# Output projection to first MLP product: four chunks ahead of the last weight tile, scale on VectorE, earlier transposes, squares put off

## The chip, the cores and the metric

The kernel runs on one core of a Trainium2 chip. The metric is the time of one execution on the device in microseconds (us), median of three runs; lower is better. The core has five engines, each with an in-order queue of its own: TensorE (PE; its weight loads are listed as PEld), VectorE (DVE), ScalarE (ACT), GpSimd (POOL) and SyncE (SP). The last three also issue DMA transfers.

## The reference, cut to what matters

One decoder layer over 1024 tokens of width 1024, float32, without batch. Three token mixers come first and are merged; the change touches only what follows them: the output projection with its residual, the norm, and the first of two MLP products.

```python
h = h + einsum('bsd,de->bse', merged, w_out)          # 1024 x 1024
hn = rms_norm(h, norm_mlp_g)                           # h * rsqrt(mean(h*h) + eps) * g
up = relu(einsum('bsd,df->bsf', hn, w_mlp_up))         # 1024 x 4096
h = h + einsum('bsf,fd->bsd', up * up, w_mlp_down)     # 4096 x 1024
return rms_norm(h, final_norm_g)
```

## The kernel before, in words

**Precision.** Every float32 product is made of three products of rounded parts: a tile is split into a high part (ScalarE, line 132) and the rest (VectorE, line 133: source minus high part), and TensorE runs high x high, high x low and low x high. So a "split" of a 128 x 1024 tile is one ScalarE and one VectorE instruction. The products are 128 x 512 matmuls into one PSUM bank.

**Order.** Inside `with tc.manual_schedule():` the program order is the order of every engine's queue. What an engine does next is therefore fixed by where the line stands in the program, whether its input is there or not. Waits between engines, and for buffers, are put in by the framework. A tile of a pool can be written once the last reader of the tile that had the buffer before is done. The pools that matter: `act2` (27 buffers of 128 x 1024, `act()`), `act3` (16), `w` (6), `raw` (2, for weights as they are loaded), `aux` and `aux2` (4 PSUM banks each).

**Output projection** (`out_products`, line 1387). The tokens are 8 chunks of 128, the output has two halves `nb` of 512 columns. A chunk and a half take 8 steps k of 3 matmuls, 24 in all. The weights of a half are four tiles `wo_make(nb, k2)` of two k each; a tile is loaded by SP into a raw buffer, and each `wo_make` also starts the load of the tile two further on. The first three tiles of half 0 are split while the merge before still runs; `wo_make(0, 3)` comes after the merge's own last work on ScalarE and VectorE. The first half goes by pairs of chunks: for the first pair k = 0..5 of both chunks, then the fourth tile is split, then k = 6, 7 of both; the three other pairs follow whole, and behind each pair one tile of half 1 is split (`wo_make(1, cp)`) and the products are added to the residual `H[c]` (line 1408). `residual(c)` loads a chunk of x; its DMA is issued on ScalarE's queue, two chunks at the start and two with each later pair.

**Second half, norm and transposes** (lines 1645 to 1667). For each chunk c: half of its matmuls; the transpose of chunk c - 2 (`transpose_plain`: eight 128 x 128 transposes on TensorE into two PSUM banks, line 1431, and eight ScalarE copies out of them with the norm's gain, line 1436); the other matmuls; for c = 5 and 6 the forms B11 and B21; the sum into `H[c]` (line 1656); `norm_scale`; the store of `H[c]` to `h_d` by POOL. `norm_scale` squares and sums the row on ScalarE (line 1414), takes the inverse root in nine tiny VectorE instructions (lines 107 to 112) and scales the row on ScalarE (line 1422). A "form" is a pair of 128 x 1024 tiles that hold a quarter of the transposed normed tokens, or a sum of quarters, and their split (`form`).

**First MLP product.** The hidden width is 16 blocks s of 2 x 128 columns. A block is a 2 x 2 product over halves of the tokens and of the inner width, done with seven products instead of eight: `p1 p2 p5 p6 p3 p7 p4`, each 12 matmuls (`seventh`, line 487). The left factors come from `Weights` (`cast1`: A11, A12; `cast12`: S1, S2; `cast34`: S3, S4; `cast22`: A22; `sums1`, `sums2` form S on VectorE, lines 511 to 516), the right ones are the forms B11, B21, B22, T1, T2, T3, T4. The products depend on one another through PSUM: p6 adds to the bank of p1, which ScalarE must have copied out before (line 1475); p3 adds to that of p5 (copy on line 1494), p7 to that of p6 (line 1498), and p4 to that of p7, whose sum VectorE must have taken (line 1509). The results lie in `o0` and `o1`, are passed through relu and a square on ScalarE (`square_relu`, lines 1452 and 1453) and stored by POOL to `u_d` together with sums of them (`sums` and `last_sum` on VectorE, lines 1515 to 1527); `last_sum` of block s comes behind p4, at the start of block s + 1.

Block 0 is done without the seven products: `plain` (line 1639) runs 24 matmuls four times (two columns, two halves of the tokens). The first token half needs B11 and B21, the second B12 and B22. Its work, and block 1, are woven by hand into the stretch in which the other forms are made:

1. plain (column 0, half 0), S sums of block 1, transpose of chunk 6
2. plain (1, 0), `cast12`, squares and store of block 0's first half, transpose of chunk 7
3. block 1's p1, forms B12 and B22, T1 difference, p2, form T1, T2 difference
4. plain (0, 1), form T2, squares of block 1's first quarter, `cast34`, T3 difference
5. plain (1, 1), form T3, T4 difference, p5, form T4, p6, first casts of block 2, squares of block 0's second half
6. p3, S sums of block 2, p7, `cast12` of block 2, block 0's sums and their stores, block 1's sums

Then the loop over s = 2..15 runs block s with p4 of block s - 1 behind its p1, and the next block's casts between its products. The second MLP product reads `u_d` back from s = 15 on.

Of the kernel before, what the change touches and what calls it, by code (L numbers as in the profile page):

```python
# [19 lines left out]
KD = D // P  # L20
# [16 lines left out]
def trunk_kernel(ctx: ExitStack, tc: tile.TileContext, x, norm_mix_g, w_in, b_gate, gmlp_ln_g, gmlp_ln_b,  # L37
# [1350 lines left out]

    with tc.manual_schedule():
        for cp in range(NCH // 2):  # L1390
            pss = [aux(), aux()]
            if cp:
                for i in range(2):
                    residual(2 * cp + i)
            if cp == 0:
                for i in range(2):
                    out_products(pss[i], 0, i, range(6))
                wo_make(0, 3)
                for i in range(2):
                    out_products(pss[i], 0, i, (6, 7))  # L1400
                wo_make(1, 0)
            else:
                for i in range(2):
                    out_products(pss[i], 0, 2 * cp + i, range(KD))
                wo_make(1, cp)
            for i in range(2):
                h = H[2 * cp + i]
                tt(out=h[:, hsl(0)], in0=pss[i], in1=h[:, hsl(0)], op=ALU.add)
# [10 lines left out]
    def norm_scale(row):  # L1419
        xn = act()  # L1420
        rs = row_rms(row, xn)
        actv(xn, row, AF.Identity, scale=rs)
        return xn
# [31 lines left out]
    class Super:  # L1455
# [33 lines left out]

        def p5(self):  # L1490
            self.b2 = aux()
            self.mul(self.b2, "S1", "T1", True)
            self.o1 = act()
            actv(self.o1[:, hsl(1)], self.b2, AF.Copy)  # L1494
# [5 lines left out]
        def p3(self):  # L1500
# [3 lines left out]
            square_relu(c)  # L1504

        def p7(self):
# [3 lines left out]
            square_relu(c)  # L1510
# [134 lines left out]
    with tc.manual_schedule():  # L1645

        xns, weights = [], {}
        for c in range(NCH):
# [4 lines left out]
            out_products(ps, 1, c, range(4, KD))  # L1653
            if c in (5, 6):
                form(("B11", "B21")[c - 5], quad(0, c - 5), act3)
            tt(out=H[c][:, hsl(1)], in0=ps, in1=H[c][:, hsl(1)], op=ALU.add)
            xns.append(norm_scale(H[c]))
            nc.gpsimd.dma_start(out=h_d[c], in_=H[c])
# [7 lines left out]
            elif c == 7:  # L1666
                weights[1].cast1()
        z0, z1 = Super(0, None), Super(1, weights[1])
# [4 lines left out]
        transpose_plain(xns[6], 6)  # L1673
        plain(z0, 1, 0, w0[1])
        weights[1].cast12()
        for o in (z0.o0, z0.o1):
            actv(o[:, hsl(0)], o[:, hsl(0)], AF.Square)
        z0.store(("A11",), z0.o0[:, hsl(0)])
        transpose_plain(xns[7], 7)
        z1.p1()  # L1680
        n11, n12, n21, n22 = quad(0, 0), quad(1, 0), quad(0, 1), quad(1, 1)
# [4 lines left out]
        for j in range(2):  # L1686
            tt(out=T1[j], in0=n12[j], in1=n11[j], op=sub)
        z1.p2(False)
        form("T1", T1, act3)
        for j in range(2):  # L1690
            tt(out=T2[j], in0=n22[j], in1=T1[j], op=sub)
        plain(z0, 0, 1, w0[0])
        form("T2", T2, act3)
        z1.square_first()
        weights[1].cast34()
        for j in range(2):
            tt(out=n12[j], in0=n22[j], in1=n12[j], op=sub)
        plain(z0, 1, 1, w0[1])
        form("T3", n12, act)
        for j in range(2):  # L1700
            tt(out=n21[j], in0=n21[j], in1=T2[j], op=sub)
        weights[2] = Weights(w_up, 4 * P, w4)
# [5 lines left out]
        for o in (z0.o0, z0.o1):  # L1708
            actv(o[:, hsl(1)], o[:, hsl(1)], AF.Square)
        z1.p3()  # L1710
        weights[2].sums1()
        weights[2].sums2()
        z1.p7()
        weights[2].cast12()
        z0.sums()
        z0.last_sum()
        z1.sums()
        weights[3] = Weights(w_up, 6 * P, w4)
        prev = z1
        dn = dn_steps()  # L1720
        for s in range(2, NS):
# [11 lines left out]
            prev.last_sum()  # L1733
# [23 lines left out]
            if last:  # L1757
                advance(dn)
            z.p7()
            if last:  # L1760
                advance(dn)
            z.sums()
            if s + 2 < NS:
# [101 lines left out]
```

## Time and profile before

| | |
|---|---|
| runs | 1957.18, 1958.79, 1960.37 us; median 1958.79 |
| profiled execution, first to last instruction | 1959.5 us, 0.7 over the median of the runs |
| mean granted TensorE clock in it | 0.991 |
| TensorE busy in it | 1905.2 us (97%) |
| VectorE, ScalarE, POOL busy | 1410.2, 1014.1, 259.3 us |

| stretch, us from the span's start | what runs | TensorE idle |
|---|---|---|
| 0 to 1212 | input projection, mixers, merge | 22.0 |
| 1212 to 1261 | output projection, first half | 2.8 |
| 1261 to 1315 | second half, norm, transposes 0 to 5 | 2.8 |
| 1315 to 1388 | plain products, blocks 1 and 2, forms | 8.3 |
| 1388 to 1927 | rest of the first MLP product, second one | 1.8 |
| 1927 to 1959.5 | last products, final norm, output | 16.6 |

The profiled execution's own time is its span; the runs' times are taken apart from it. In the rows, a line of the timeline gives the start, the length, the engine, the program line, the operation, what it writes and reads, the count, and in brackets the idle time before it with what ended it. Tiles are named by their pool: `a` is `act2`, `b` is `act3`, `wt` and `wb` are `w`, `rt` is `raw`. A matmul of 512 columns is listed with about 389 ns, but a new one starts every 227 ns at the full clock; a listed busy stretch of TensorE ends some 0.16 us after the next instruction could have started.

### The profile page before, as it was taken

The page shows a single profiled execution, that of the slowest core. Times are in us where ns is not written, and L with a number is a line of the kernel's source. Part 1 is how long each engine was busy: PE and PEld are TensorE (multiplying, and loading weights), DVE is VectorE, ACT ScalarE, POOL GpSimd, SP SyncE. Part 2 cuts the span into 40 slices and gives each one's busy share as a digit, 9 for nine tenths or more (in the row PEclk, how much of TensorE's full clock was granted, in tenths as well). Part 3 has the DMA queues.
Part 4 walks back from the last instruction along what each step waited for, and adds up shares of the span by engine and source line. Part 5 has one row for each costly group of instructions (what it writes and reads, how often), then busy time and mean ns, then how long its engine had stood idle before and what let it go on. Part 6 is the DMA issues. An engine that isn't in the chain of part 4 may idle for free.

```text
span 1959.5 us, 23757 instructions
## 1 busy us (share of the span) xinstructions
PE 1905.2 (97%) x8928; PEld 1587.5 (81%) x8928; DVE 1410.2 (72%) x2039; ACT 1014.1 (52%) x1471; POOL 259.3 (13%) x355
## 2 busy tenths in 40 slices
PE   8999999999999999999999999998999999999996
PEld 7998878888887787878778887877788887888885
DVE  6585869788758767677777888248655567688787
ACT  6435959676534545454554544167555556243253
POOL 3112112122342010100010110000211110000000
PEclk9999999999999999999999999999999999999998
DMA  4346475576754343434497986331544448453532
GB/s 162 75 137 145 110 153 122 121 164 138 169 142 136 107 151 108 151 108 129 149 287 256 279 220 194 107 108 54 199 139 167 154 172 294 164 172 118 183 119 86
DMA packets 211015, 301.25 MB, mean 154 GB/s; under 512 B 13028, under 2 KB 125876, under 8 KB 210900
## 3 DMA queue, kind: packets, MB, share of 16 engines
q1 hardware_dynamic: 167348, 158.54, 26.4%
q0 software_dynamic: 34544, 119.69, 22.8%
q10 hardware_dynamic: 9008, 21.51, 3.1%
q8 instruction: 70, 1.15, 0.3%
q14 instruction: 45, 0.37, 0.1%
HBM read 195.75 MB, written 74.58 MB: 138 GB/s over the span
## 4 chain that ended last, share of the span: by engine, by line
PE 74%; DVE 9%; issue 6%; ACT 5%; DMA 5%; POOL 1%; ACTq 0%; POOLq 0%; DVEq 0%; SPq 0%
PE aux L487 39%; PE ps L564 14%; PE gps L487 10%; PE aux L257 4%; PE aux L1387 2%; PE aux L800 1%; DMA a<-acs_d 1%; DMA c<-yc_d 1%; ACT a L1436 1%; DMA raw<-in_w_in_dram 1%; PE aux L736 1%; PE aux L732 1%; DVE a L133 1%; DVE rsq_q L111 1%; ACT a L132 1%
## 5 line engine op out<-in xcount | busy, mean ns | idle before, releaser
L564 PE MATMUL ps<-xn,wh 128*128 128x512 f32 x1088 | 295.0, 392 | 0.0
L487 PE MATMUL aux<-b,b 128*128 128x512 f32 x1152 | 264.4, 389 | 1.0 <-DVE b L133 0.9
L487 PEld LDWEIGHTS aux<-b,b 128*128 128x128 f32 x1152 | 216.0, 188 | 47.0 <-DVE b L133 1.8
L564 PEld LDWEIGHTS ps<-xn,wh 128*128 128x128 f32 x1088 | 202.9, 188 | 42.2 <-issue 0.9
L487 PE MATMUL aux<-a,b 128*128 128x512 f32 x960 | 219.4, 389 | 0.0
L487 PEld LDWEIGHTS aux<-a,b 128*128 128x128 f32 x960 | 180.2, 188 | 37.4
L564 PE MATMUL ps<-xn,wl 128*128 128x512 f32 x544 | 168.2, 389 | 0.0
L487 PE MATMUL gps<-xn,wt 128*128 128x512 f32 x684 | 160.2, 392 | 2.1 <-DVE a L238 2.1
L487 PE MATMUL aux<-b,wt 128*128 128x512 f32 x672 | 156.9, 389 | 0.0
L487 PEld LDWEIGHTS gps<-xn,wt 128*128 128x128 f32 x684 | 129.4, 189 | 29.5 <-issue 2.5
L487 PEld LDWEIGHTS aux<-b,wt 128*128 128x128 f32 x672 | 126.1, 188 | 26.2
L132 ACT ACTIVATE b<-wt 128x1024 fp32r<-128x1024 f32 x88 | 90.8, 1052 | 86.4 <-DMA wt<-u_d 51.9
L133 DVE TENSOR_TENSOR wt<-a,wt 128x1024 fp32r<-128x1024 f32 x66 | 80.8, 1225 | 66.9 <-ACT wt L132 66.9
L564 PEld LDWEIGHTS ps<-xn,wl 128*128 128x128 f32 x544 | 102.1, 188 | 21.4
L133 DVE TENSOR_TENSOR b<-wt,b 128x1024 fp32r<-128x1024 f32 x88 | 107.1, 1218 | 15.8 <-ACT b L132 15.8
L1617 DVE TENSOR_TENSOR a<-aux,a 128x512 f32<-128x512 f32 x112 | 76.9, 687 | 50.2 <-PE aux L487 50.2
L133 DVE TENSOR_TENSOR a<-a,a 128x1024 fp32r<-128x1024 f32 (+1 forms) x68 | 66.6, 985 | 41.5 <-ACT a L132 41.5
L133 DVE TENSOR_TENSOR wt<-rt,wt 128x1024 fp32r<-128x1024 f32 x35 | 42.8, 1224 | 57.2 <-ACT wt L132 57.0
L132 ACT ACTIVATE a<-a 128x1024 fp32r<-128x1024 f32 (+1 forms) x68 | 55.9, 837 | 54.1 <-DVE a L1569 45.9
L487 PE MATMUL aux<-a,wt 128*128 128x512 f32 x336 | 78.7, 390 | 3.3 <-ACT a L1494 3.3
L487 PEld LDWEIGHTS aux<-a,wt 128*128 128x128 f32 x336 | 62.9, 188 | 17.2 <-ACT a L1494 4.2
L132 ACT ACTIVATE wt<-a 128x1024 fp32r<-128x1024 f32 x66 | 69.6, 1055 | 8.7 <-DVE a L515 8.3
(349 smaller groups left out, 3521.2 us busy)
## 6 DMA issues: line engine op xcount, KB each, us to landing
wt<-u_d SPq DMA_DIRECT2D x54, 512.0 KB
u_d<-a POOLq DMA_DIRECT2D x48, 512.0 KB, 5.3
raw<-in_w_in_dram SPq DMA_DIRECT2D x34, 512.0 KB
wl<-raw POOLq DMA_DIRECT2D x34, 512.0 KB, 5.1
g_d<-a POOLq DMA_DIRECT2D x24, 512.0 KB, 3.3
a<-g_d ACTq DMA_DIRECT2D x24, 512.0 KB
rt<-in_w_in_dram SPq DMA_DIRECT2D x19, 512.0 KB
a<-in_w_in_dram SPq DMA_DIRECT2D x19, 512.0 KB
```

Of the source, the lines that this page charges most:

```text
L111: stt(out=q, in0=r, scalar=nh, in1=r, op0=ALU.mult, op1=ALU.mult)
L132: actv(dst_hi, src, AF.Copy)
L133: (eng or nc.vector).tensor_tensor(out=dst_lo, in0=src, in1=dst_hi.bitcast(F32), op=ALU.subtract)
L257: mm(ps[:, :nt], X.tok(a, k, c), wk[k][w], start=(k == 0 and i == 0), stop=(k == KD - 1 and i == 2))
L487: mm(ps, lhs[l][kk], rhs[r][kk], start=(new and n == 0), stop=(n == 11), skip_group_check=not new)
L564: mm(ps[:, hsl(h)], w[wi][:, k, :], a.rhs(ai, k, h), start=(n == 0), stop=(n == 3 * KD - 1))
L732: mm(yo[:, tok(i)], pv[c // 2][:, c % 2, j * P:(j + 1) * P], Cf[:, tok(c)], start=True, stop=True)
L736: mm(yi[64 * h:64 * h + 64, tok(i)], xdt[c // 2][:, c % 2, 2 * j + h, :], E[c // 2][:, c % 2, 2 * j + h, :], start=True, stop=True)
L800: mm(ps, w[wi][:, q * P:(q + 1) * P], S["xs"][half][ai], start=(n == 0), stop=(n == 2))
L1387: mm(ps, M.tok(a, k, c), wo[nb][k][w], start=(k == 0 and a + w == 0), stop=(k == KD - 1 and a == 1))
L1436: actv(Nf[th, k // 2][:, k % 2, (c % 4) * P:(c % 4 + 1) * P], ps[:, i * P:(i + 1) * P], AF.Identity, scale=g2c[:, KD + k:KD + k + 1])
L1617: tt(out=h, in0=ps, in1=h, op=ALU.add)
```

## The change

- First half of the projection: residual chunks 2 and 3 are loaded at once. k = 0..5 runs for four chunks, then `wo_make(0, 3)`, then k = 6, 7 of each of the four with its sum and the load of residual c + 4; then `wo_make(1, 0)`; chunks 4 to 7 follow singly, with `wo_make(1, 1..3)` ahead of the sums of chunks 4 to 6.
- `norm_scale`: the scaling by the inverse root is a VectorE `tensor_scalar` instead of a ScalarE activation.
- Second half: sum, norm and store stand ahead of the forms B11 and B21. Transpose 6 moves ahead of the first plain product, transpose 7 ahead of the second.
- Block 1: the forms B12 and B22 and the T1 difference come ahead of p1; T1, T2 and `cast34` ahead of plain (0, 1); T3 and the T4 difference ahead of plain (1, 1).
- The squares of blocks 0 and 1, the store of A11 of both, and both blocks' `sums` and `last_sum` leave the stretch. A generator `catch_up` gives them out in six parts, two in each of the blocks s = 2, 3 and 4: one ahead of p7, one behind `sums`. Only p4's own relu and square of block 1 stay where they were.

```diff
@@ -1386,26 +1386,28 @@
             for a, w in ((0, 0), (0, 1), (1, 0)):
                 mm(ps, M.tok(a, k, c), wo[nb][k][w], start=(k == 0 and a + w == 0), stop=(k == KD - 1 and a == 1))
 
+    def add_half(c, nb, ps):
+        tt(out=H[c][:, hsl(nb)], in0=ps, in1=H[c][:, hsl(nb)], op=ALU.add)
+
     with tc.manual_schedule():
-        for cp in range(NCH // 2):
-            pss = [aux(), aux()]
-            if cp:
-                for i in range(2):
-                    residual(2 * cp + i)
-            if cp == 0:
-                for i in range(2):
-                    out_products(pss[i], 0, i, range(6))
-                wo_make(0, 3)
-                for i in range(2):
-                    out_products(pss[i], 0, i, (6, 7))
-                wo_make(1, 0)
-            else:
-                for i in range(2):
-                    out_products(pss[i], 0, 2 * cp + i, range(KD))
-                wo_make(1, cp)
-            for i in range(2):
-                h = H[2 * cp + i]
-                tt(out=h[:, hsl(0)], in0=pss[i], in1=h[:, hsl(0)], op=ALU.add)
+        for c in (2, 3):
+            residual(c)
+        pss = [aux() for _ in range(4)]
+        for c in range(4):
+            out_products(pss[c], 0, c, range(6))
+        wo_make(0, 3)
+        for c in range(4):
+            out_products(pss[c], 0, c, (6, 7))
+            add_half(c, 0, pss[c])
+            residual(c + 4)
+        wo_make(1, 0)
+        for c in range(4, NCH):
+            ps = aux()
+            out_products(ps, 0, c, range(KD))
+            if c < 7:
+                wo_make(1, c - 3)
+            add_half(c, 0, ps)
+    del pss, ps
 
     Nf = {}
 
@@ -1419,7 +1421,7 @@
     def norm_scale(row):
         xn = act()
         rs = row_rms(row, xn)
-        actv(xn, row, AF.Identity, scale=rs)
+        ts(out=xn, in0=row, scalar1=rs, scalar2=None, op0=ALU.mult)
         return xn
 
     def transpose_plain(xn, c):
@@ -1487,6 +1489,10 @@
             square_relu(c)
             self.store(("A11",), c)
 
+        def square_rest(self):
+            square_relu(self.o0[:, hsl(1)])
+            square_relu(self.o1[:, hsl(1)])
+
         def p5(self):
             self.b2 = aux()
             self.mul(self.b2, "S1", "T1", True)
@@ -1497,17 +1503,19 @@
             self.mul(self.b1, "S2", "T2", False)
             actv(self.o0[:, hsl(1)], self.b1, AF.Copy)
 
-        def p3(self):
+        def p3(self, square=True):
             self.mul(self.b2, "S4", "B22", False)
             c = self.o0[:, hsl(1)]
             tt(out=c, in0=self.b2, in1=c, op=ALU.add)
-            square_relu(c)
-
-        def p7(self):
+            if square:
+                square_relu(c)
+
+        def p7(self, square=True):
             self.mul(self.b1, "S3", "T3", False)
             c = self.o1[:, hsl(1)]
             tt(out=c, in0=self.b1, in1=c, op=ALU.add)
-            square_relu(c)
+            if square:
+                square_relu(c)
 
         def sums(self):
             self.s12, self.s34 = act(), act()
@@ -1651,11 +1659,11 @@
             if c >= 2:
                 transpose_plain(xns[c - 2], c - 2)
             out_products(ps, 1, c, range(4, KD))
+            add_half(c, 1, ps)
+            xns.append(norm_scale(H[c]))
+            nc.gpsimd.dma_start(out=h_d[c], in_=H[c])
             if c in (5, 6):
                 form(("B11", "B21")[c - 5], quad(0, c - 5), act3)
-            tt(out=H[c][:, hsl(1)], in0=ps, in1=H[c][:, hsl(1)], op=ALU.add)
-            xns.append(norm_scale(H[c]))
-            nc.gpsimd.dma_start(out=h_d[c], in_=H[c])
             if c == 0:
                 w0 = plain_weights()
             elif c in (1, 2):
@@ -1665,59 +1673,69 @@
                 weights[1] = Weights(w_up, 2 * P, act)
             elif c == 7:
                 weights[1].cast1()
+        transpose_plain(xns[6], 6)
         z0, z1 = Super(0, None), Super(1, weights[1])
         z0.o0, z0.o1 = act(), act()
         plain(z0, 0, 0, w0[0])
         weights[1].sums1()
         weights[1].sums2()
-        transpose_plain(xns[6], 6)
+        transpose_plain(xns[7], 7)
         plain(z0, 1, 0, w0[1])
+        n11, n12, n21, n22 = quad(0, 0), quad(1, 0), quad(0, 1), quad(1, 1)
         weights[1].cast12()
-        for o in (z0.o0, z0.o1):
-            actv(o[:, hsl(0)], o[:, hsl(0)], AF.Square)
-        z0.store(("A11",), z0.o0[:, hsl(0)])
-        transpose_plain(xns[7], 7)
-        z1.p1()
-        n11, n12, n21, n22 = quad(0, 0), quad(1, 0), quad(0, 1), quad(1, 1)
         form("B12", n12, act)
         form("B22", n22, act)
         T1 = [act((P, 2, HF)) for _ in range(2)]
         T2 = [act((P, 2, HF)) for _ in range(2)]
         for j in range(2):
             tt(out=T1[j], in0=n12[j], in1=n11[j], op=sub)
+        z1.p1()
+        form("T1", T1, act3)
         z1.p2(False)
-        form("T1", T1, act3)
         for j in range(2):
             tt(out=T2[j], in0=n22[j], in1=T1[j], op=sub)
+        form("T2", T2, act3)
+        weights[1].cast34()
         plain(z0, 0, 1, w0[0])
-        form("T2", T2, act3)
-        z1.square_first()
-        weights[1].cast34()
         for j in range(2):
             tt(out=n12[j], in0=n22[j], in1=n12[j], op=sub)
-        plain(z0, 1, 1, w0[1])
         form("T3", n12, act)
         for j in range(2):
             tt(out=n21[j], in0=n21[j], in1=T2[j], op=sub)
+        plain(z0, 1, 1, w0[1])
         weights[2] = Weights(w_up, 4 * P, w4)
         z1.p5()
         form("T4", n21, act)
         z1.p6()
         weights[2].cast1()
         weights[1].cast22()
-        for o in (z0.o0, z0.o1):
-            actv(o[:, hsl(1)], o[:, hsl(1)], AF.Square)
-        z1.p3()
+        z1.p3(False)
         weights[2].sums1()
         weights[2].sums2()
-        z1.p7()
+        z1.p7(False)
         weights[2].cast12()
-        z0.sums()
-        z0.last_sum()
-        z1.sums()
         weights[3] = Weights(w_up, 6 * P, w4)
+
+        def catch_up():
+            z1.square_first()
+            z1.square_rest()
+            yield
+            z1.sums()
+            z1.last_sum()
+            yield
+            for o in (z0.o0, z0.o1):
+                actv(o[:, hsl(0)], o[:, hsl(0)], AF.Square)
+            z0.store(("A11",), z0.o0[:, hsl(0)])
+            yield
+            for o in (z0.o0, z0.o1):
+                actv(o[:, hsl(1)], o[:, hsl(1)], AF.Square)
+            yield
+            z0.sums()
+            yield
+            z0.last_sum()
+
         prev = z1
-        dn = dn_steps()
+        dn, late_work = dn_steps(), catch_up()
         for s in range(2, NS):
             last = s == NS - 1
             nxt = weights.get(s + 1)
@@ -1730,7 +1748,8 @@
                 dn_rows(0, act)
                 dn_weights(0, "B22", r4)
             prev.p4()
-            prev.last_sum()
+            if s > 2:
+                prev.last_sum()
             if last:
                 advance(dn)
             z.p2()
@@ -1756,10 +1775,12 @@
                 nxt.cast22()
             if last:
                 advance(dn)
+            advance(late_work)
             z.p7()
             if last:
                 advance(dn)
             z.sums()
+            advance(late_work)
             if s + 2 < NS:
                 weights[s + 2] = Weights(w_up, 2 * (s + 2) * P, w4)
             elif s + 2 == NS:
```

## The prediction

> **What bounds the kernel now.** I read the windows by stage first, then TensorE's timeline in the stage that changes, then the other queues at each gap.
>
> ```profile
> 1212.00:1261.00 49.00, 46.20 (x196) 37.55 (x195) 20.19 (x22) 9.92 (x10) 0.00 (x0) 0.97 0.44 150
> 1261.00:1315.00 54.00, 51.20 (x241) 41.93 (x240) 21.77 (x69) 30.61 (x66) 3.78 (x7) 0.97 0.25 88
> 1315.00:1388.00 73.00, 64.70 (x279) 51.38 (x277) 54.49 (x76) 45.43 (x77) 6.47 (x10) 0.98 0.35 112
> 1388.00:1927.00 539.00, 537.17 (x2367) 444.16 (x2368) 381.08 (x451) 249.54 (x326) 37.47 (x55) 1.00 0.48 163
> 1355.00:1356.00 1.00, 1.00 (x4) 0.76 (x3) 1.00 (x1) 0.00 (x0) 0.00 (x0) 0.50 0.00 0
> ```
>
> Columns: busy us of PE, weight load, DVE, ACT, POOL, then granted clock. From 1388 to 1927 us TensorE is almost never idle, so whatever TensorE saves before 1388 reaches the end. In the three stages before it is idle 2.8, 2.8 and 8.3 us, and at times it runs at half clock (last row, just after a wait). The change touches these stages alone. Its matmuls and transposes stay the same in number, so the result is decided by these gaps.
>
> ```profile
> 1212.01 8.32 PE L1387 MATMUL aux<-wb,b 128*128 128x512 f32 x36
> 1221.44 0.50 PE L1387 MATMUL aux<-a,b 128*128 128x512 f32 x1 [1.10 <-ACT a L132]
> 1223.64 4.03 PE L1387 MATMUL aux<-a,b 128*128 128x512 f32 x11 [1.70 <-DVE a L133]
> 1280.47 1.03 PE L1431 MATMUL aux<-ident,a 128*128 128x128 f32 x8
> 1286.81 1.03 PE L1431 MATMUL aux<-ident,a 128*128 128x128 f32 x8
> 1308.68 0.66 PE L1431 MATMUL aux<-ident,a 128*128 128x128 f32 x4 [2.35 <-ACT a L1436]
> 1314.55 5.62 PE L1639 MATMUL aux<-b,wt 128*128 128x512 f32 x24
> 1354.27 7.70 PE L487 MATMUL aux<-a,a 128*128 128x512 f32 x24 [2.71 <-ACT a L1494]
> 1388.02 3.02 PE L487 MATMUL aux<-a,a 128*128 128x512 f32 x12 [0.26 <-DVE a L1509]
> 1399.04 5.60 PE L487 MATMUL aux<-a,wt 128*128 128x512 f32 x24
> 1404.48 2.88 PE L487 MATMUL aux<-b,wt 128*128 128x512 f32 x12
> 1260.70 0.69 DVE L1408 TENSOR_TENSOR a<-aux,a 128x512 f32<-128x512 f32 x1 [4.75 <-PE aux L1387]
> ```
>
> Prices of TensorE from starts: 24 matmuls take 1404.48 - 1399.04 = 5.44, so a burst of 12 takes 2.72 and one matmul 0.227. A chunk of the second half with its transpose takes 1286.81 - 1280.47 = 6.34, so a transpose of a chunk costs 0.90.
>
> Losses against these prices. *A*, first half of the projection: 192 matmuls from 1212.01 should end at 1255.5; the last sum of it starts at 1260.70, so it ended near 1260.5: lost 5.0 (two gaps, the drain before them, and the half clock that follows). *B*, second half: 8 x 5.44 + 6 x 0.90 = 48.9 from 1260.5 gives 1309.4; the plain products start at 1314.55: lost 5.1. *C*, from there to 1388.02: 96 plain matmuls (21.8), two transposes (1.8) and 14 bursts (38.1) make 61.6 of 73.5: lost 11.8. All together 21.9: the most that can be won, if nothing new waits.
>
> **The change, part by part.**
>
> *A, four chunks ahead.*
>
> ```profile
> 1220.35 1.99 ACT L132 ACTIVATE a<-rt 128x1024 fp32r<-128x1024 f32 x2
> 1222.37 2.35 DVE L133 TENSOR_TENSOR a<-rt,a 128x1024 fp32r<-128x1024 f32 x2
> 1216.84 1.88 ACTq L1372 DMA_DIRECT2D a<-in_x_dram  x1
> 1228.49 1.23 DVE L133 TENSOR_TENSOR a<-rt,a 128x1024 fp32r<-128x1024 f32 x1
> 1238.01 1.06 ACT L132 ACTIVATE a<-rt 128x1024 fp32r<-128x1024 f32 x1 [7.63 <-DMA rt<-in_w_out_dram]
> ```
>
> TensorE has 36 matmuls before it needs the last weight tile, which is split at 1220.35 on ScalarE and ready near 1223.6 on VectorE. With four chunks it has 72: 16.3 us, until 1228.3. Slack 4.7. The loads of residual chunks 2 and 3 now stand ahead of that split on ScalarE's queue: up to 1.9 us each to issue, and if they get the buffers that the split's own tiles had, these are free by 1222.4 at the latest; the tile is then ready by about 1225.2, still early. The later residual loads depend on no product; if one waits for a buffer, only wo_make(1, 0) is behind it on ScalarE, and that is not urgent: on VectorE it now goes behind four sums, which end with TensorE's fourth chunk at 1228.3 + 5.4, so near 1235 instead of 1223. Each later weight load waits on SP for the raw buffer that a split frees. The last one went out when the split at 1228.49 was done and was taken by ScalarE at 1238.01, 8.3 later. Now it goes out near 1237, so its tile is split by 1248; it is first read at 1255.5 + 18 x 0.227 = 1259.6. Behind it on SP, the first weights of the MLP product start to load some 4 earlier or as late as before; they are split after 1268. Nothing waits: **5.0 won**, second half from 1255.5.
>
> *B, sum and norm ahead of the forms, scale on VectorE.*
>
> ```profile
> 1300.30 2.36 DVE L133 TENSOR_TENSOR b<-a,b 128x1024 fp32r<-128x1024 f32 x2 [4.29 <-ACT b L132]
> 1302.58 0.68 DVE L1656 TENSOR_TENSOR a<-aux,a 128x512 f32<-128x512 f32 x1
> 1303.30 1.06 ACT L1414 ACTIVATE a<-a 128x1024 f32<-128x1024 f32 x1 [2.08 <-DVE a L1656]
> 1306.45 1.15 ACT L1422 ACTIVATE a<-a,rs 128x1024 f32<-128x1024 f32 x1 [2.00 <-DVE rs L112]
> 1307.50 2.16 ACT L1436 ACTIVATE a<-aux,g2c 128x128 f32<-128x128 f32 x8
> L328 DVE TENSOR_SCALAR a<-a,rsx 128x1024 f32<-128x1024 f32 x4 | 3.6, 910 | 1.9 <-POOL rsx L126 1.8
> L1802 DVE TENSOR_SCALAR a<-a,roots 128x512 f32<-128x512 f32 x1 | 0.5, 486 | 0.0
> ```
>
> Chunk 5's sum stands on VectorE behind the form's split, which waits for ScalarE: 1302.58, though its products ended near 1286.81 + 6.34 + 0.90 + 2.72 = 1296.8. The norm, its scale and the previous chunk's copies out of PSUM (1307.50) follow, and TensorE waits 2.35. In the new order a chunk is ready 0.2 (which I take from the end of the products to VectorE's start), 0.7 (sum, 1302.58 to 1303.30), 3.15 (square and root, to 1306.45) and the scale after its products. The scale now costs VectorE between 0.5 (half a row) and 0.91; I take 0.86, near the whole-row one; ScalarE saves 1.15. That is 4.9, and the transpose of a chunk stands 8 us behind its products. The store of the sum on POOL now goes ahead of the forms too; nothing is behind it there. From 1255.5, chunk 5 ends at 1291.8 and its form is split until 1299.0; chunk 6 ends 1298.1, is scaled by 1303.7; chunk 7 ends 1304.45. Its transpose of chunk 6 follows at once; one PSUM buffer comes free at 1304.9: 0.2 lost. Chunk 7's sum waits for the second form (1306.1), so it is scaled by 1310.8; the plain product covers that until 1311.0: 0.1 lost. **4.8 won.**
>
> *C, the chain of forms.*
>
> ```profile
> 1332.71 3.95 ACT L132 ACTIVATE a<-a 128x1024 fp32r<-128x1024 f32 x4
> 1333.86 4.63 DVE L133 TENSOR_TENSOR a<-a,a 128x1024 fp32r<-128x1024 f32 x4 [3.31 <-ACT a L132]
> 1379.95 0.68 DVE L511 TENSOR_TENSOR a<-a 128x512 f32<-128x512 f32 x1
> 1380.55 0.68 DVE L512 TENSOR_TENSOR a<-rt,a 128x512 f32<-128x512 f32 x1
> 1376.54 0.63 ACT L1452 ACTIVATE a<-a 128x512 f32<-128x512 f32 x1 [5.71 <-DVE a L1481]
> 1378.68 0.58 ACT L1494 ACTIVATE a<-aux 128x512 f32<-128x512 f32 x1
> L1452 ACT ACTIVATE a<-a 128x512 f32<-128x512 f32 x45 | 28.4, 632 | 83.8 <-DVE a L1481 33.8 <-DVE a L1503 27.4 <-DVE a L1509 22.5
> ```
>
> A whole tile costs VectorE 4.63/4 = 1.16, half of one 0.60; ScalarE 0.95 and some 0.6. ScalarE works in order, so the chain starts once the second plain product's output (PE 1317.35) is taken: cast12 at 1318.1, VectorE from 1319.1. Up to the last T3 tile VectorE has 16 whole tiles (cast12, cast34, two each for B12, B22, the sums T1, T2, T3 and the forms T1, T2) and p2's half: 16 x 1.16 + 0.6, 1338.2. ScalarE splits it, takes the plain output and copies p5 by 1340.4. TensorE has meanwhile run p1, p2, both plain products (moved back, they now cover the forms T1 and T2), p5 and p6 until 1339.1: p3 waits 1.3. p1's copy, now behind four splits on ScalarE, is done near 1323, long before p6 needs it. Four more tiles to T4 (1342.9), its split and p6's copy end at 1344.5: p7 waits 1.4 and ends at 1347.3. p7's sum comes behind two T4 splits, two casts, p3's sum and four weight sums: 1350.95; with z2.p1 between, p4 waits 1.0. Then, where L1494 came late at 1378.68 because VectorE was busy with z0's and z1's sums (5.71 idle ahead of L1452), those sums are gone and p5's copy is in time.
>
> *The work put off.* It comes back at s = 2 to 4: on ScalarE six relu and squares (3.8) ahead of p7, then four squares (2.5); on VectorE eight half sums (4.8); all with their five stores on POOL, which is busy 37.5 of 539 us. ScalarE is busy 249.5 of 539 us and VectorE 381.1, so most lies in their free time. The bounds are nothing and the 8.6 that is ahead of something on a queue; walking the queues gives 0.4 (p3 at s = 3, behind ScalarE), 0.5 and 0.9 (p4, whose sum is behind others on VectorE): 1.9 with rounding.
>
> C loses 1.3 + 1.4 + 1.0 + 1.9 = 5.6 instead of 11.8: **6.2 won.** No new wait is over 1.4 us, and a whole burst lies between any two, so I add no half clock.
>
> **Sum.** 5.0 + 4.8 + 6.2 = 16.0 from a span of 1959.5 gives 1943.5; the median of the runs shown is 0.7 under that span: **1943**.
>
> **The rivals.**
>
> *The half clock isn't the gaps' doing.* If it came from elsewhere, three stretches of 3.4 us at half speed stay, 1.7 each: 5.1 less, 1948. Against it: the row at 1355 shows 0.50 right behind a wait of 2.71, and 1388 to 1927 shows 1.00. [...]
>
> *The second block's weights come late.*
>
> ```profile
> 1344.91 0.37 SPq L497 DMA_DIRECT2D a<-in_w_mlp_up_dram  x1
> SPq L497 <- DVE a L1691: 58.4, 1, 58.4
> 1351.00:1353.00 2.00, 0.56 (x3) 0.14 (x1) 2.00 (x3) 1.38 (x2) 0.00 (x0) 1.00 0.00 0
> ```
>
> This load waits for a buffer that T2's subtraction frees; no DMA moves from 1351 on, so it lands in 6. Its sums come at 1347.9 in the new order. Freed by T2 (1331) it is early; freed only by the last T4 tile (1345) it is 3.3 late, VectorE holds p7's sum behind it, and one wait of 4.3 brings a half clock: 5.0 more, 1948.
>
> *The forms take as long as before.* Only A and B win: 1949.
>
> *Everything fits.* No wait is left: 1958.8 - 21.9 = 1937.
>
> *Slower: the tiles run out.* z0's and z1's tiles are held longer. At the end of s = 2 I count 12 of the pool's 27 for the forms, 3 for weights, 2 for z0, 4 each for z1 and z2 and 1 loading: 26. If a block's first output tile must then wait for a store to land, ScalarE stands, and TensorE behind it.
>
> ```profile
> u_d<-a POOLq DMA_DIRECT2D x48, 512.0 KB, 5.3
> ```
>
> A wait of 5.3 brings a half clock, 1.7. Two such blocks leave a gain of 2; with all three (s = 2, 3, 4) it is 1943 + 21 = 1964, slower. Against it: followed through the pool in the program's order, the tile that a block gets first was left over two bursts before.
>
> **How the numbers follow.** Chances: forecast 0.58; everything fits 0.10; late weights 0.10; half clock 0.06; forms as long 0.06; slower by the tiles 0.05; the gains only move to later waits, no difference, 0.05. A measurement here tells 0.2% (3.9 us) from none. The range from 1937 to 1951 holds all but the last two and what exceeds their prices. Faster 0.90, same 0.05, slower 0.05.
>
> **What would show it.** A: no gap in 96 matmuls from 1212, second half near 1255.5. B: no form ahead of L1656's counterpart, plain products near 1305.5. C: waits of 1 to 1.4 before p3, p7, p4, clock 1.00 throughout, z2.p4 about 18 earlier. The forecast is wrong if a single new wait over 2 us stands in s = 2 to 4.

## The result, and the profile after

The changed kernel takes 1942.24 us (median of four runs, 1941.91 to 1944.10); the kernel before, on the same chip, 1958.26. The ratio is 0.9919, with an interval of 0.9907 to 0.9931. The prediction was 1943, in a range of 1937 to 1951.

TensorE's timeline of the changed kernel, the rows that answer to those shown of before (start, length, engine, line, what it writes and reads, count, idle time before it):

```profile
1208.96 16.48 PE L1387 MATMUL aux<-wb,b 128*128 128x512 f32 x72
1225.28 5.60 PE L1387 MATMUL aux<-a,b 128*128 128x512 f32 x24
1266.08 1.04 PE L1433 MATMUL aux<-ident,a 128*128 128x128 f32 x8
1301.40 1.03 PE L1433 MATMUL aux<-ident,a 128*128 128x128 f32 x8
1302.19 5.70 PE L1647 MATMUL aux<-b,wt 128*128 128x512 f32 x24
1330.38 5.60 PE L487 MATMUL aux<-b,a 128*128 128x512 f32 x24
1337.03 3.02 PE L487 MATMUL aux<-a,a 128*128 128x512 f32 x12 [1.05 <-ACT a L1500]
1341.17 3.06 PE L487 MATMUL aux<-a,a 128*128 128x512 f32 x12 [1.12 <-ACT a L1504]
1347.80 3.00 PE L487 MATMUL aux<-a,a 128*128 128x512 f32 x12 [0.86 <-DVE a L1516]
1366.96 2.88 PE L487 MATMUL aux<-a,a 128*128 128x512 f32 x12
1378.39 5.74 PE L487 MATMUL aux<-a,wt 128*128 128x512 f32 x24 [0.39 <-ACT a L1500]
1387.11 3.02 PE L487 MATMUL aux<-a,a 128*128 128x512 f32 x12 [0.26 <-DVE a L1516]
1407.05 3.02 PE L487 MATMUL aux<-a,a 128*128 128x512 f32 x12 [0.60 <-DVE a L1516]
```

The two gaps of the first half and the 2.35 ahead of a transpose are gone; the 2.71 ahead of block 1's p3 is down to 1.05, and the wait ahead of block 2's p3, 2.56 before, is gone. Six small waits are left in the first product: p3, p7 and p4 of block 1, then one ahead of p3 and two ahead of p4 in blocks 3 and 4. Two rows of before that the text below compares with, the third and fourth plain products and p3 of block 2:

```profile
1335.13 10.99 PE L1639 MATMUL aux<-a,wt 128*128 128x512 f32 x47 [0.76 <-DVE a L133]
1379.31 5.74 PE L487 MATMUL aux<-a,wt 128*128 128x512 f32 x24 [2.56 <-ACT a L1494]
```

The windows of after by stage (busy us of PE, weight load, DVE, ACT, POOL, then the granted clock) say the same:

```profile
1212.00:1256.00 44.00, 44.00 (x196) 36.44 (x195) 17.56 (x19) 9.94 (x10) 0.00 (x0) 1.00 0.47 165
1256.00:1305.00 49.00, 49.00 (x246) 41.16 (x245) 29.09 (x87) 28.28 (x71) 4.30 (x8) 1.00 0.32 112
1305.00:1370.00 65.00, 61.97 (x275) 50.43 (x274) 48.96 (x59) 39.59 (x65) 1.09 (x2) 1.00 0.22 62
1370.00:1411.00 41.00, 39.75 (x173) 31.96 (x172) 28.82 (x40) 23.33 (x37) 9.75 (x15) 1.00 0.62 199
```

TensorE is never idle in the first two stages, 3.03 in the third (1.05 + 1.12 + 0.86) and 1.25 in the fourth (0.39 + 0.26 + 0.60), and the clock is full in all four.

To compare kernels whose projection starts at different times, I cut each profile by three rows: the start of the projection, the first transpose, the first plain product, and the end of the span. The stages are called by the prediction's letters. A: 1208.96 to 1266.08, five bursts of 12 matmuls of the second half included. B: from there to 1302.19. C: from there to the end, 1940.5. Before (and where the early transposes are left out) the seventh transpose of a chunk stands behind the first plain product; there 0.90 is moved from C to B.

| kernel | start | A | B | C | start to end |
|---|---|---|---|---|---|
| before | 1212.01 | 62.09 | 41.35 | 644.05 | 747.49 |
| after | 1208.96 | 57.12 | 36.11 | 638.31 | 731.54 |
| won | 3.05 | 4.97 | 5.24 | 5.74 | 15.95 |

The 3.05 ahead of the projection isn't counted as the change's, since nothing was changed there. It is taken up below.

### The profile page after: what moved, and what is told of

Read it like the earlier page. It is cut to its first block, busy times and chain, and to the rows that moved or that the text cites. A ratio compares the mean times of both kernels' runs of the same rounds, so it can differ in the third digit from the quotient of the medians.

```text
span 1940.5 us, 23747 instructions
## 1 busy us (share of the span) xinstructions
PE 1895.9 (98%) x8928; PEld 1581.8 (82%) x8928; DVE 1415.9 (73%) x2047; ACT 1005.3 (52%) x1463; POOL 259.0 (13%) x355
## 3 DMA queue, kind: packets, MB, share of 16 engines
q8 instruction: 70, 1.15, 0.2%
## 4 chain that ended last, share of the span: by engine, by line
PE 81%; DVE 9%; issue 4%; ACT 3%; DMA 3%; POOL 1%; ACTq 0%; SPq 0%; POOLq 0%; DVEq 0%
PE aux L487 40%; PE ps L564 16%; PE gps L487 11%; PE aux L1387 4%; PE aux L257 4%; PE aux L800 1%; DMA raw<-in_w_in_dram 1%; PE aux L736 1%; PE aux L732 1%; DVE wt L133 1%; ACT wt L132 1%; PE aux L712 1%; PE aux L1647 1%; DVE a L133 1%; PE aux L847 0%
## 5 line engine op out<-in xcount | busy, mean ns | idle before, releaser
L133 DVE TENSOR_TENSOR wt<-a,wt 128x1024 fp32r<-128x1024 f32 x66 | 80.8, 1225 | 65.1 <-ACT wt L132 65.0
```

What stands on the lines that cost most here:

```text
L133: (eng or nc.vector).tensor_tensor(out=dst_lo, in0=src, in1=dst_hi.bitcast(F32), op=ALU.subtract)
```

## The experiments

Each kernel below was run beside the kernel before on one chip. The chips differ between some rows of the table, so compare ratios and stages there, not medians. Two of the kernels are repeats, without an edit. Before again:

> The kernel before, profiled once more. In the two profiles so far the output projection begins at 1212.0 us before and 1209.0 after the change, 3.0 apart, though nothing ahead of it was changed. If that is a matter of the execution, this profile begins it at another time than 1212.0, between 1208 and 1213, and the span follows it; from there on the same gaps as before: TensorE idle 1.1 and 1.7 near the last weight tile, 2.35 before the transpose of chunk 5, 2.7 before block 1's p3 and 2.6 before block 2's p3. If the change moved the stage ahead of it (by another layout of buffers), it begins at 1212 again within 0.5.

It took 1961.2, with the same gaps to 0.1, one more of 0.17 ahead of block 1's p7, and half-clock stretches at the same three places. Its projection begins at 1211.86, within 0.5 of 1212: by the expectation this speaks for a shift that the change itself brings. After again:

> The kernel after once more, for comparison on the same chip as the two kernels that change it further: 1942.2, and in its profile the same waits of 1.05, 1.12 and 0.86 at p3, p7 and p4 of block 1 and 0.39, 0.26 and 0.60 at s = 3 and 4.

It took 1944.23, ratio 0.9916 (0.9902 to 0.9931), with the same six waits to 0.03. Its projection begins at 1210.51, that of the same kernel's first profile at 1208.96: so one program starts this stage 1.55 apart in two executions, and the repeat of before alone doesn't decide the question. The last section says how much stays open. The others, with stages as above:

| kernel | median us | ratio to before (interval) | A | B | C |
|---|---|---|---|---|---|
| four ahead only | 1955.49 | 0.9978 (0.9969 to 0.9987) | 57.12 | 39.76 | 646.68 |
| after without four ahead | 1947.05 | 0.9936 (0.9924 to 0.9948) | 62.10 | 36.11 | 638.27 |
| the same, wait filled | 1946.84 | 0.9936 (0.9924 to 0.9949) | 60.53 | 36.10 | 638.31 |
| scale back on ScalarE | 1949.13 | 0.9944 (0.9932 to 0.9957) | 57.12 | 41.21 | 639.77 |
| forms ahead of the sum | 1945.44 | 0.9928 (0.9916 to 0.9941) | 57.12 | 37.76 | 638.31 |
| nothing put off | 1947.42 | 0.9935 (0.9922 to 0.9949) | 57.12 | 36.11 | 642.45 |
| relu behind the forms | 1939.39 | 0.9890 (0.9874 to 0.9907) | 57.13 | 36.10 | 634.40 |
| the same, late work spread | 1936.94 | 0.9879 (0.9865 to 0.9894) | 57.12 | 36.10 | 632.19 |

**Stage A by itself.** Before, with only the new loop over chunks of the first half:

```diff
-        for cp in range(NCH // 2):
...
+        pss = [aux() for _ in range(4)]
+        for c in range(4):
+            out_products(pss[c], 0, c, range(6))
+        wo_make(0, 3)
...
```

> The kernel before with the new first half of the output projection alone. Queue theory (TensorE is the limit there; its waits and the half clock behind them are all that is lost): 5.0 less than before, 1953.3, with the first half taking 43.5 us from its first matmul to the last sum instead of 48.7, and the gaps of the later stages unchanged. Rival, gains move: the later stages are set by ScalarE and VectorE, which start no earlier, so what is won is lost again by 1388 us and the time stays at 1958. Rival, the half clock is not the waits' doing: 3.3 less, 1955, and a stretch at 0.5 remains in the first half.

And after, with the old loop (the reverse of this edit):

> The kernel after with the old first half of the output projection (two chunks ahead). Queue theory: 5.0 more than after, 1947.2; the wait for the last weight tile is back (1.1 and 1.7), the clock falls to 0.5 for 3.4 us behind it, and nothing later changes. Rival, the parts overlap (the later stages hide part of it): under 3 more. Rival, the half clock is not the waits' doing: 3.3 more.

Taken out of after, the part costs 62.10 - 57.12 = 4.98, all in A. Put into before, it wins the same 4.97 in A and less in all: 3.5 by the medians, and 3.9 from the start of the projection to the end (747.49 against 743.56), not the 5.0 that was expected. Timeline of that kernel, then windows of it and of before, two on either side of the same wait of 2.56:

```profile
1327.87 12.57 PE L1641 MATMUL aux<-a,wt 128*128 128x512 f32 x47 [0.76 <-DVE a L133]
1372.05 7.38 PE L487 MATMUL aux<-a,wt 128*128 128x512 f32 x24 [2.56 <-ACT a L1496]
```
```profile
1368.90:1372.20 3.30, 0.74 (x4) 0.32 (x3) 1.00 (x2) 2.89 (x5) 1.27 (x2) 1.00 0.98 265
1372.40:1375.60 3.20, 3.20 (x9) 2.49 (x8) 2.87 (x5) 1.07 (x2) 0.00 (x0) 0.50 1.08 392
```
```profile
1375.10:1378.40 3.30, 1.65 (x8) 1.03 (x6) 1.41 (x3) 1.83 (x3) 1.62 (x3) 1.00 1.03 317
1378.50:1381.90 3.40, 2.59 (x11) 2.17 (x12) 3.06 (x5) 1.27 (x4) 0.18 (x1) 1.00 1.04 329
```

B is 1.59 shorter too (39.76 against 41.35), but only because the half clock that before has ahead of the first plain product, at 1310.22, now comes in the third and fourth, in C: there 47 matmuls take 12.57 instead of 10.99. Counted from the start of the projection, p3 of block 2 comes 5.0 earlier (1379.31 - 1212.01 = 167.30 before, 1372.05 - 1209.74 = 162.31 here). There the wait of 2.56, which no half clock followed in before, is followed by one: 24 matmuls take 7.38 instead of 5.74. The half-clock stretches of before begin on a grid of 3.41 (last section). In before the same wait lies across two steps of that grid (the rows above show 1.65 and 0.81 idle; in the grid's own steps it is 1.74 and 0.82), here all 2.56 lie in the 3.30 shown just ahead of the stretch. So the later waits came to lie elsewhere on the grid, and 1.6 of the gain went to the stretch. Before's wait of 0.26 ahead of the next p4 (1388.02) doesn't come here, which gives 0.5 back, and 3.9 is left.

**How much of A is half clock.** After without four ahead, with 14 matmuls more in the wait for the last weight tile. They write a PSUM bank that nothing reads:

```diff
                 wo_make(0, 3)
+                fill = aux()
+                for i in range(14):
+                    mm(fill, M.tok(0, i % 6, 0), wo[0][i % 6][0], start=True, stop=True)
```

> As the kernel after with the old first half, but with 14 matmuls on ready operands into a spare PSUM bank (their result is not used) in TensorE's queue where it waits for the last weight tile; they take 14 x 0.227 = 3.2 us, the length of the wait. They do no work of use and do not shorten the wait. If the wait itself brings the half clock: no stretch at 0.5 there, and 1.7 less than with the open wait, so 1945.5 (3.3 over after). If the half clock comes from something else: it stays, and the time is that of the kernel with the open wait, 1947.2.

Windows at the same place, without the filling and with it:

```profile
1221.70:1224.90 3.20, 3.20 (x9) 2.44 (x8) 0.85 (x2) 0.59 (x1) 0.00 (x0) 0.50 0.78 283
```
```profile
1221.70:1224.90 3.20, 3.20 (x15) 2.40 (x14) 2.72 (x3) 0.00 (x0) 0.00 (x0) 1.00 0.28 100
```

With the wait as long as before but TensorE busy, the half clock doesn't come, and A falls from 62.10 to 60.53: of the 5.0, 1.6 are the half clock and 3.4 the gaps and the drains before them. The medians of the two kernels (1946.84 and 1947.05) don't tell 1.6 apart; the stage does.

**Stage B: the scale's engine, and the place of the forms.** Each undone by itself in after:

```diff
-        ts(out=xn, in0=row, scalar1=rs, scalar2=None, op0=ALU.mult)
+        actv(xn, row, AF.Identity, scale=rs)
```

> The kernel after with the norm's scale back on ScalarE; all else as after. Queue theory, walking the queues with the rows of the two profiles: ScalarE cannot go on to the next form's splits and PSUM copies until VectorE has the root (2.0) and the scale is done (1.15), and this adds up over chunks 5 to 7: TensorE waits 1.7 at the transpose of chunk 5, 4.8 at that of chunk 6 and 1.1 at that of chunk 7, all for PSUM banks that ScalarE has yet to copy out; 7.6 more than after, 1950, and up to 1.7 more if the clock falls. Rival, that the engine is a trifle because a transpose stands 8 us behind its chunk's products (which is how the prediction told it): within 1 of after, 1942 to 1943.

```diff
+            if c in (5, 6):
+                form(("B11", "B21")[c - 5], quad(0, c - 5), act3)
             add_half(c, 1, ps)
...
-            if c in (5, 6):
-                form(("B11", "B21")[c - 5], quad(0, c - 5), act3)
```

> The kernel after with the forms B11 and B21 ahead of the sum and the norm again, the scale staying on VectorE. Queue theory: the sum of chunks 5 and 6 comes late on VectorE; by the walk only the transpose of chunk 6 waits, 2.0 for its scaled rows: 2.0 more than after, 1944.2, 3.7 more if that wait brings the half clock. Rival, that the order of forms and sum was the main cost of the second half (as the prediction put it first): 4 to 5 more, 1947.

With the scale on ScalarE nearly all of B's gain is gone: 41.21 against 36.11, and a half clock in the plain product behind it (7.18 for 24 matmuls) costs 1.5 more in C. That is 6.6 in all, where 7.6 and up to 1.7 for the clock were expected: chunk 6's transpose waits 3.15, not 4.8, and chunk 7's not at all. With the forms first, 1.65 is lost, of 2.0 expected. ScalarE's timeline of the kernel with the scale on ScalarE, TensorE's longest wait there and the plain product behind it, and TensorE's one wait in the second half with the forms first:

```profile
1287.74 1.15 ACT L1424 ACTIVATE a<-a,rs 128x1024 f32<-128x1024 f32 x1 [2.01 <-DVE rs L112]
1293.98 1.15 ACT L1424 ACTIVATE a<-a,rs 128x1024 f32<-128x1024 f32 x1 [2.00 <-DVE rs L112]
1302.27 1.15 ACT L1424 ACTIVATE a<-a,rs 128x1024 f32<-128x1024 f32 x1 [2.00 <-DVE rs L112]
1310.54 1.15 ACT L1424 ACTIVATE a<-a,rs 128x1024 f32<-128x1024 f32 x1 [2.00 <-DVE rs L112]
```
```profile
1306.38 0.92 PE L1433 MATMUL aux<-ident,a 128*128 128x128 f32 x4 [2.26 <-ACT a L1438]
1306.95 7.18 PE L1647 MATMUL aux<-b,wt 128*128 128x512 f32 x24
```
```profile
1307.18 1.10 PE L1433 MATMUL aux<-ident,a 128*128 128x128 f32 x8 [1.44 <-DVE a L1424]
```

The reason can be read off the spacing. TensorE takes 6.34 for a chunk. With the scale on it, ScalarE squares a row, stands 2.00 until VectorE has the inverse root, scales, and copies: without a form 1293.98 - 1287.74 = 6.24, just within. A form adds two splits, and a chunk takes 1302.27 - 1293.98 = 8.29: two chunks with a form put ScalarE 3.9 behind, and its copies out of PSUM with it. With the scale on VectorE, ScalarE needn't wait for the root. ScalarE's and VectorE's rows of after:

```profile
1296.46 1.06 ACT L1416 ACTIVATE a<-a 128x1024 f32<-128x1024 f32 x1 [1.66 <-DVE a L1390]
1303.27 1.06 ACT L1416 ACTIVATE a<-a 128x1024 f32<-128x1024 f32 x1 [1.71 <-issue]
1314.26 0.60 ACT L1650 ACTIVATE a<-aux 128x512 f32<-128x512 f32 x1 [3.67 <-PE aux L1647]
1314.75 3.89 ACT L132 ACTIVATE a<-a 128x1024 fp32r<-128x1024 f32 x4
```
```profile
1292.80 0.75 DVE L1424 TENSOR_SCALAR a<-a,rs 128x1024 f32<-128x1024 f32 x1
1315.84 2.36 DVE L133 TENSOR_TENSOR a<-a,a 128x1024 fp32r<-128x1024 f32 x2 [5.05 <-ACT a L132]
```

Chunks with a form now take 6.81 (1303.27 - 1296.46) instead of 8.29, and for 1.7 of that ScalarE is idle. Neither part was put into before by itself, and the earlier transposes weren't taken out by themselves. The rows from 1314 on belong to stage C, below.

**Stage C: the work put off.** After, with the squares, stores and sums of blocks 0 and 1 back at their old places among the products:

```diff
+        for o in (z0.o0, z0.o1):
+            actv(o[:, hsl(0)], o[:, hsl(0)], AF.Square)
+        z0.store(("A11",), z0.o0[:, hsl(0)])
...
-        z1.p3(False)
+        z1.p3()
...
+        z0.sums()
+        z0.last_sum()
+        z1.sums()
```

> The kernel after with the squares, stores and sums of blocks 0 and 1 back where they stood before among the forms; the new order of the forms stays. Queue theory: p3 of block 1 waits 2.5 instead of 1.1, p3 of block 2 waits 2.7 again (VectorE holds both blocks' sums ahead of p2's), the first plain product of the second half 0.8; the waits at s = 3 and 4 (2.0 in all) go: 3.2 more than after, 1945.4, and up to 3.4 more where a wait over 1.7 brings the half clock on. Rival, putting off only moves the cost: within 1 of after.

```profile
1338.84 3.01 PE L487 MATMUL aux<-a,a 128*128 128x512 f32 x12 [2.90 <-ACT a L1500]
1363.34 7.35 PE L487 MATMUL aux<-a,wt 128*128 128x512 f32 x24 [2.58 <-ACT a L1500]
```
```profile
1364.90:1368.10 3.20, 3.20 (x9) 2.52 (x8) 2.77 (x4) 1.06 (x1) 0.00 (x0) 0.50 0.93 352
```

Putting off is worth 4.1 in C: p3's wait is 2.90 instead of 1.05, block 2's p3 waits 2.58, and a half clock follows that one (7.35 for 24 matmuls). None followed the wait of 2.90 (12 matmuls in 3.01); counted back in steps of 3.41 from the stretch shown, that wait lies across two steps, some 1.6 and 1.3 in each. The wait of 0.8 that was expected ahead of a plain product didn't come. Of the 5.7 won in C, 1.6 is left over; the new order of forms, which would have to bring it, was not taken out by itself.

**What is left, and a better version.** In after the chain of forms starts on ScalarE at 1314.75, behind the relu that takes the second plain product's output (1314.26, idle 3.67 before it). VectorE is idle for 5.05 until the first high part of that chain (`cast12`'s, ahead of the forms) is there. So I had that one relu issued behind the forms B12 and B22:

```diff
-        plain(z0, 1, 0, w0[1])
+        relu10 = plain(z0, 1, 0, w0[1])
...
         form("B22", n22, act)
+        relu10()
```

> The kernel after with one ScalarE instruction moved: the relu of the second plain product goes behind the forms B12 and B22. In the profile of the kernel after ScalarE stands idle 3.7 us for that product and VectorE 5.0 behind it, at the head of the chain of forms that p3, p7 and p4 later wait for. Queue theory: the chain starts near 1311 instead of 1315.8, the waits of block 1's p3 (1.05), p7 (1.12) and p4 (0.86) go with their drains (0.16 each), the three at s = 3 and 4 stay: 3.5 less than after, 1938.7. Rival, the chain is not what these products wait for, or the weights of block 2 (loaded late) take its place: within 1 of after.

ScalarE's and VectorE's timeline of that kernel:

```profile
1311.91 4.92 ACT L132 ACTIVATE a<-a 128x1024 fp32r<-128x1024 f32 x5
1316.66 0.65 ACT L1649 ACTIVATE a<-aux 128x512 f32<-128x512 f32 x1
```
```profile
1313.06 5.77 DVE L133 TENSOR_TENSOR a<-a,a 128x1024 fp32r<-128x1024 f32 x5 [0.78 <-ACT a L132]
```

Counted from the start of the projection the chain begins 4.3 earlier (1311.91 - 1210.44 = 101.47, against 1314.75 - 1208.96 = 105.79), and none of the waits ahead of p3, p7 and p4 of block 1 is left: 3.9 less in C, and 4.8 less by the medians beside after again (1944.23). Expected was 3.5. On top of it, the work put off was spread over four blocks, with fewer squares at once:

```diff
             z1.square_first()
-            z1.square_rest()
+            yield
+            square_relu(z1.o0[:, hsl(1)])
+            yield
+            square_relu(z1.o1[:, hsl(1)])
             yield
...
+            yield
             z0.sums()
-            yield
             z0.last_sum()
```

> As the kernel with the relu behind the forms, and the work put off spread over s = 2 to 5 in smaller parts: two quarters of block 1 at s = 2, the third and block 1's sums at s = 3, block 0's squares at s = 4, its sums at s = 5 behind the block's own. Queue theory: also the waits at s = 3 (p3 0.39, p4 0.26) and s = 4 (p4 0.60) go, so TensorE has no gap from the projection's start to the second product: 5.4 less than after, 1936.8, which is the 21.9 in all that the prediction counted as lost. Rival, the put-off work costs something wherever it stands, or tiles held longer bring new waits: no gain over the kernel with the relu moved alone.

Its windows at the places that showed waits in after:

```profile
1305.00:1370.00 65.00, 65.00 (x293) 53.91 (x292) 52.47 (x65) 41.49 (x67) 3.26 (x5) 1.00 0.25 76
1370.00:1411.00 41.00, 41.00 (x183) 33.94 (x182) 25.80 (x36) 26.22 (x40) 8.70 (x13) 1.00 0.65 208
```

TensorE is never idle in the windows where after lost 3.03 and 1.25. Another 2.2 is won, and from the start of the projection to the end it is 725.41, 22.1 less than before: the prediction's "21.9: the most that can be won". At 1936.94 this is the fastest version, 7.3 under after on the same chip.

## Why the prediction was right, point by point

**A, 5.0 won: right.** A lost nothing: 252 matmuls at 0.2267 make 57.12, to the hundredth what the row of the first transpose gives. The weight tile's two splits were in time, and no load behind them came late. That 1.6 of it is the half clock, which the prediction counted into that loss ("the half clock that follows"), is shown by the filled wait.

**B, 4.8 won: 5.2 measured, but its reason was told wrongly.** The waits of 0.2 and 0.1 didn't come; the scale took 0.75 on VectorE, not 0.86. The size is near because it is the measured loss of 5.1 less 0.3, whatever the reason for that loss. The step that failed is the explanation: "Chunk 5's sum stands on VectorE behind the form's split", with the scale entering only as 1.15 against 0.86 in the time of a chunk. The runs put 5.1 on the scale's engine and 1.65 on the place of the forms. What I missed is that ScalarE, in order, stands 2.00 for the root in every chunk; moving the scale frees 3.15 of its period, not 0.3 of a latency. The two parts overlap: together they won 5.2. The row "[2.00 <-DVE rs L112]" was quoted in the prediction and not read as a period.

**C, 6.2 won: 5.7 measured.** The waits forecast at 1.3, 1.4 and 1.0 were 1.05, 1.12 and 0.86, each at its place. The chain's start, forecast 12.6 behind the first plain product, came 12.56 behind it. With the drain and refill around each (p3 starts 1337.03, 24 matmuls at 1330.38 would have allowed 1335.82: 1.21 for a wait of 1.05) these three cost 3.9, by the relu behind the forms, not 3.7. The late work cost 2.2, by the spread version, where the walk along the queues gave 1.9; its waits of 0.39, 0.26 and 0.60 were forecast 0.4, 0.5 and 0.9. The "bounds" of nothing and 8.6 would have said little; the walk did. Block 2's p4 was to come "about 18 earlier": counted from the start of the projection it does (1388.02 - 1212.01 = 176.01 before, 1366.96 - 1208.96 = 158.00 after).

**No half clock: right.** After's granted clock is 1.00 from 610.35 to 1927.89. No wait left in the changed stages is over 1.12; the least idle time in one step of the grid that a stretch followed in before is 1.70, ahead of 1224.89. That "a whole burst lies between any two" was needed as well is not shown; with it, the most that one step holds in after from 1212 to 1411 is 1.05. The rival that the half clock comes from elsewhere is out: in these stages it left with the gaps, and in A it left with a filled wait.

**The rivals.** The second block's weights: the load was issued early, at 1328.04, behind T2's subtraction. SyncE's and VectorE's rows of after:

```profile
1328.04 0.37 SPq L497 DMA_DIRECT2D a<-in_w_mlp_up_dram  x1
```
```profile
1326.75 2.35 DVE L1696 TENSOR_TENSOR a<-a,a 128x1024 f32<-128x1024 f32 x2
```

That tiles run out wasn't seen: none of TensorE's waits in blocks 2 to 4 is over 0.6. "Everything fits" isn't true of this change, which leaves six waits; the last version, another kernel, reaches it, at 1936.94 where the rival said 1937. "The forms take as long as before" and "the gains only move" are out with the 5.7 won in C.

**The bridge to the time: right by luck.** The sum 16.0 was right (15.95), with B's 0.4 over the forecast against C's 0.5 under it. But the profiled span of before was taken as the execution's own time, 0.7 above the median. An execution takes 1.7 more than its span (after: 1942.18 and 1940.5; before again: 1961.2 and 1959.5), so by that the one profiled took about 2.4 more than the median. The excess seems to have lain ahead of the projection, where 3.05 fell away; no profile of a median execution of before shows it. From 1943.5, minus 3.05, plus 1.7, comes 1942.15; the prediction took off 0.7 and got 1942.8.

## What to carry to other kernels

Read an in-order engine by its period for one chunk beside the period of the engine that it feeds: an instruction of 1.15 that stands behind a 2.00 wait for another engine costs 3.15 of every period, and moving it to the engine that makes its input took both away here. Gains of parts didn't add up here where waits near 2 us were left behind: measure a part by taking it out of the whole as well as by putting it in alone, and compare stages cut by rows, which tell 1.6 apart where medians of whole runs don't. When waits are left, follow the chain back to its first instruction: here the place of one relu of 0.6 at its head cost 3.9.

## What the runs showed of the hardware

**The half-clock stretches begin on a grid of 3.41.** In before those of the changed stages begin at 1224.89, 1310.22 and 1354.59, which are 25 and 13 steps of 3.413 apart, and each is 3.41 long. The same program met the grid at another place in its repeat: there the first of them begins near 1224.3 (granted clock 0.82 from 1223 to 1225), 0.6 earlier, and the projection 0.15 earlier. With the grid laid over TensorE's idle times from 10 to 1900 us, six steps of before were followed by a stretch (1.98, 2.03, 2.10, 1.70, 2.25 and 2.71 idle, in order of time) and two of after (2.08 and 2.36). Of the steps that none followed, the most idle are 1.74 and 1.65 in before and 1.62 in after: 1.70 and 1.74 went one each way. None followed the wait of 2.56 in before, nor that of 2.90 with nothing put off, each of which lies across two steps. What sets a stretch off was not shown beyond these numbers.

**What lies ahead of the projection.** Windows at the same early place, in before and in after, where the program is the same:

```profile
40.60:43.80 3.20, 3.20 (x13) 3.20 (x12) 2.58 (x9) 2.42 (x8) 3.20 (x4) 0.50 0.00 0
```
```profile
40.60:43.80 3.20, 3.20 (x23) 3.18 (x23) 2.38 (x9) 2.17 (x7) 3.20 (x4) 1.00 0.03 8
```

Before, with a stretch there, starts the projection at 1212.01, after, without one, at 1208.96. With the forms first there is one there and one near 283 (granted clock 0.50 from 281.7 to 284.9), and the projection starts at 1213.15. The starts of all twelve profiles lie between 1208.62 and 1213.15. So 3.05 of the 19 us between the spans of before and after lie ahead of the projection. By the 1.6 that a stretch cost in the first product (7.38 against 5.74), the early one is about half of that, an estimate. Whether the rest is the change's or the execution's stays open, and what decides whether the early stretch comes was not tried.
